# Attention scores of a three-block network: second product over all 128 partitions, index and retention heads issued in pairs

## The chip, the cores and the metric

The kernel runs on one core of a Trainium2 chip. The metric is the device time of one launch in microseconds (us). Before the change three runs took 3308.53, 3309.18 and 3311.11 us; the median is 3309.18.

## What is computed

Three blocks of a network over 512 tokens of 1024 features, batch 1, in float32. The first is a mixer with a linear recurrence, a gated MLP over chunks and a convolutional feed-forward part. The second holds an mLSTM and a differential attention. The third is a gated feed-forward part, a hybrid mixer of three branches (retention, sparse attention, memory attention) and another feed-forward part. The change touches these pieces of the second and third block:

```python
logits = jnp.einsum('bhmqd,bhmkd->bhmqk', qh[:, :, :, q0:end], kh[:, :, :, :end])   # diff_attention, 8 heads x 2 maps, 64 features
p = jax.nn.softmax(logits + bias[None, :, None], axis=-1)
a = p[:, :, 0] - lam * p[:, :, 1]
...
scores = jnp.einsum('bnihd,bnjhd->bnhij', qc, kc) * decay_in[None, None]             # retention, 4 heads, 64 features
...
rel = jax.nn.relu(jnp.einsum('bqhd,bsd->bqhs', qib, ki).astype(jnp.float32))         # index of the sparse attention, 8 heads, 64 features
score = jnp.einsum('bqhs,bqh->bqs', rel, wib.astype(jnp.float32))
_, idx = lax.top_k(score, topk)                                                      # 128 keys per query
logits = jnp.einsum('bqhd,bqkhd->bhqk', qb, k_sel).astype(jnp.float32) * scale       # sparse attention, 8 heads, 64 features
```

## The kernel before

**Parts of a number.** TensorE multiplies float32r numbers, so every float32 operand is split into a high part (ScalarE rounds it) and a low part (VectorE subtracts), and a product is hi·hi + hi·lo + lo·hi, three matmuls into one PSUM tile: `mm3` (L495, L496, L497) for two activations, `dense` (L419, L420, L422) and `dense_n` (L438 to L440) for an activation and a weight. Weights come by DMA 128x1024 at a time and are split on the way: L102 on ScalarE gives `whi`, L107 on VectorE gives `wlo`. Tokens lie along the free dimension, in tiles of [128 features, 512 tokens].

**Heads of 64 features.** A tile of 128 features holds two heads. `stack` prepares them for `product`: on the left ("sl") the head's own 64 partitions hold the high part and the other 64 the low part; on the right ("sr") both halves hold the high part, and the low part is in a tile of its own, "srl" [128, 512], head 0 on partitions 0 to 63 and head 1 on 64 to 127. `product` then needs two matmuls: L532 over 128 partitions gives hi·hi + lo·hi, L533 over the head's 64 partitions adds hi·lo. Two loops use it: `diff_attn` (8 heads, 4 query blocks, 2 maps: 64 products) and `dsa_branch` (4 pairs, 2 halves, 4 query blocks: 32 products). A query block has 128 queries against 256, 256, 384 and 512 keys. After a product VectorE adds the bias and finds the maximum (L1352), ScalarE takes the exponential (L1354), VectorE divides (L1448 to L1450, or L1792 and L1793), TensorE transposes the weights (L1382), ScalarE and VectorE split them (L1390, L1391), and `attn_pv` multiplies them with the values by `mm3`. In `dsa_branch` GpSimd adds the mask to the bias (L1789). `qk_part` makes the stacked q and k of the next head, or of the next pair, from two `dense` products; in `dsa_branch` it is called after half 0 of a pair and stands in the queues beside half 1.

**Index and retention.** `dsa_index` has 8 heads in 4 tiles (m = 0 to 3) and three query blocks for each: 24 times `mm3` over 64 partitions; ScalarE applies the relu (L1722, into "rl") and VectorE sums over the heads (L1725, L536). `ret_branch` has 4 heads and four key blocks for each, 512, 384, 256 and 128 columns wide: 16 times `mm3` over 64 partitions; VectorE multiplies with the decay (L1658) and the result is split into "Ph" and "Pl".

**Order.** Each engine runs its own queue in the order that a scheduler fixed when the program was built; it weighs the dependences, so that `dense` matmuls of later work stand between the steps of an attention head. An instruction waits until the tiles that it reads are written and the buffer that it writes is free. PSUM has 8 banks: 4 buffers "mm" for the dense products and 4 buffers "sd" for scores, transposes, sums over partitions and value products.

Of the kernel before, what the change touches and what calls it, by code (L numbers as in the profile page):

```python
# [9 lines left out]
FT = mybir.dt.float32  # L10
# [6 lines left out]
P = 128  # L17
# [34 lines left out]
class VecLayout:  # L52
    """Columns of the packed [128, n] array of small vectors."""
# [21 lines left out]
class Stream:  # L75
    """Weight tiles in the order in which TensorE takes them, split into two float32r parts."""
# [46 lines left out]
    def prime(self):  # L123
        """Starts the first load."""
# [11 lines left out]
    def get(self, name, k, c0, again=False):  # L136
        """The next tile of the stream, or with again one that is still held."""
# [31 lines left out]
class Act:  # L169
    """An activation in T-layout: hi and lo parts per 128 features, [128, n] each."""  # L170
# [17 lines left out]
class Norm:  # L188
    """Sums over the features of a residual stream that comes tile by tile, then the normalised tiles."""
# [19 lines left out]
    def adder(self, cols):  # L209
        """The engine that adds the tile up: what is close to the end goes to the faster one."""  # L210
# [8 lines left out]
    def warm(self):  # L219
        """Has the table of Sqrt loaded before it is waited for."""  # L220
        self.nc.scalar.activation(self.small(), self.named("q")[:, 0:2], AF.Sqrt)

    def post(self, cols):
        """What may wait until the next products run."""
# [11 lines left out]
    def mod(self, x, k, r, gs, sh, h, cols):  # L236
        """h = x * r * gs + sh, in two parts"""
# [6 lines left out]
    def mod_off(self, x, k, r, gs, sh, h, cols):  # L244
        """mod without VectorE"""
# [9 lines left out]
class NormMod(Norm):  # L255
    """x is kept in DRAM; rms norm, gain, modulation"""
# [53 lines left out]
class NormGain(Norm):  # L310
    """x = rms norm (gain g), kept in DRAM"""
# [20 lines left out]
class NormLayer(Norm):  # L332
    """x = layer norm, kept in DRAM; the mean of tile 0 comes off before the sums are taken"""
# [41 lines left out]
class Kernel:  # L375
# [7 lines left out]
    # ---------------------------------------------------------------- helpers  # L383
# [14 lines left out]
    def xh(self, dt=FT):  # L398
        """One of the [128, 512] slots of the residual stream and its normalised form."""
# [13 lines left out]
    def dense(self, name, c0, K, parts, k0=0, again=False, ks=None):  # L413
        """parts: [(psum, Act)]; psum[m, t] = sum_k w[k, c0 + m] act[k, t]; ks: the part of the k to do now."""
# [9 lines left out]
    def dense_group(self, jobs, a):  # L424
        """jobs: [(psum, name, c0, K)]: the first half of the tokens for all, then the second."""
# [5 lines left out]
    def dense_n(self, name, c0, K, a, pss, ks=None):  # L431
        """pss[b][t, m] = sum_k act[k, 128 b + t] w[k, c0 + m], m < 512."""
# [55 lines left out]
    def last_of(self, engine):  # L488
        """The last instruction so far of an engine."""
# [19 lines left out]
    def stack(self, pool, src, left, bufs=None):  # L509
        """The two heads of src[128, T] (64 features each) for product(): their columns follow each other.  # L510

        left: hi on the head's own partitions, lo on the other half. Otherwise hi on both halves,
        and lo in a tile of its own."""
        nc = self.nc
        a = self.t(pool, [P, 2 * T], "sl" if left else "sr", FR, bufs)
        lo = a if left else self.t(pool, [P, T], "srl", FR, bufs)
        for i in range(2):
# [5 lines left out]
            else:  # L523
                nc.vector.tensor_sub(lo[r, :], src[r, :], a[r, c].bitcast(FT))
                nc.vector.tensor_copy(a[o, c], a[r, c].bitcast(FT))
        return a if left else (a, lo)

    def product(self, ps, l, lc, r, rc, i):
        """ps = l[:, lc]^T r[:, rc] over the features of head i, l and r as stack() makes them."""
        s, mm = slice(64 * i, 64 * i + 64), self.nc.tensor.matmul  # L530
        lc, rl = slice(i * T + lc.start, i * T + lc.stop), slice(i * T + rc.start, i * T + rc.stop)
        mm(ps, l[:, lc], r[0][:, rl], start=True, stop=False)  # L532
        mm(ps, l[s, lc], r[1][s, rc], start=False, stop=True)  # L533
# [4 lines left out]
    def colsum(self, src, cols=FULL):  # L538
        """PSUM [128, n]: the sum over partitions, on every partition."""
# [4 lines left out]
    def rsqrt(self, pool, src, scale, eps, tag="t"):  # L544
        """1 / sqrt(scale * src + eps)"""
# [13 lines left out]
    def log1p_exp_neg_abs(self, pool, y, shape, tag):  # L559
        """log(1 + exp(-|y|)) by 2 atanh(e / (2 + e))."""  # L560
# [17 lines left out]
    # ---------------------------------------------------------------- the residual stream  # L578
# [9 lines left out]
    def keep_x(self, k, cols):  # L588
        """x[k] goes to DRAM, which is where the next residual sum takes it from."""
# [5 lines left out]
    def next_x(self):  # L595
        """x of the last norm becomes the old x."""
# [3 lines left out]
    def residual(self, alloc, scale):  # L600
        """An epilogue: x[m] = psum * scale(m) + old x[m]."""
# [10 lines left out]
    # ---------------------------------------------------------------- whole  # L612
# [1349 lines left out]
```

## Time and profile before

| | |
|---|---|
| three runs | 3308.53, 3309.18, 3311.11 us |
| profiled execution, span from first to last instruction | 3311.8 us |
| TensorE busy | 3227.9 us, 97% |
| VectorE busy | 2038.7 us, 62% |
| ScalarE busy | 1312.3 us, 40% |
| GpSimd busy | 190.9 us, 6% |
| chain that ended last | 82% TensorE, 10% VectorE, 3% DMA, 2% ScalarE |
| mean granted clock of TensorE | 0.987 |

The only time recorded of the profiled execution itself is its span, 2.6 us above the median of the runs. The span of TensorE's work in `diff_attn` is about 1568 to 1792 us, in `dsa_index` 2376 to 2406, in `ret_branch` 2570 to 2639, and in `dsa_branch` 2719 to 2815. A matmul's duration in the trace is that of one passing through the array; matmuls overlap, so what one costs in a stream is the distance from its start to the start of the next.

### The profile page before, as it was taken

How to read it: one execution, taken by the hardware profiler on the slowest of the kernel's cores; microseconds unless marked ns; L12 is line 12 of the kernel's file. 1: busy time of each engine (PE TensorE's matmuls, PEld its weight loads, DVE VectorE, ACT ScalarE, POOL GpSimd, SP SyncE). 2: the span in 40 equal slices, each digit the busy share in tenths (PEclk: the TensorE clock that was granted, in tenths of full speed). 3: DMA queues.
4: the chain of work that ended last, by engine and by line, in shares of the span. 5: the costliest groups of instructions: out<-in, count | busy, mean ns of one | idle time of the engine just before them, and what ended most of it. 6: DMA issues, size and time to landing. Idle time of an engine off the chain costs nothing.

```text
span 3311.8 us, 40039 instructions
## 1 busy us (share of the span) xinstructions
PE 3227.9 (97%) x15534; PEld 2651.9 (80%) x15534; DVE 2038.7 (62%) x3160; ACT 1312.3 (40%) x2010; POOL 190.9 (6%) x264
## 2 busy tenths in 40 slices
PE   8999999999999999999999999999999999989998
PEld 4778788888888888887777888888887777788887
DVE  6996676588738746655777353333796647563334
ACT  4665232344324433433655233222543535342222
POOL 2100000100001000000000010000200002020001
PEclk9999999999999999999999999999999999999999
DMA  5124766433333232232222333333323131333331
GB/s 202 51 64 135 242 219 190 132 98 100 105 111 98 70 102 89 65 101 86 67 86 69 113 115 102 102 109 102 116 81 117 54 109 61 115 103 98 109 109 61
DMA packets 123108, 352.52 MB, mean 106 GB/s; under 512 B 13978, under 2 KB 28668, under 8 KB 122788
## 3 DMA queue, kind: packets, MB, share of 16 engines
q1 hardware_dynamic: 118612, 336.18, 32.2%
q0 software_dynamic: 4304, 13.77, 1.3%
q8 instruction: 122, 2.00, 0.2%
q14 instruction: 70, 0.57, 0.1%
HBM read 337.27 MB, written 16.82 MB: 107 GB/s over the span
## 4 chain that ended last, share of the span: by engine, by line
PE 82%; DVE 10%; DMA 3%; issue 2%; ACT 2%; SPq 0%; POOL 0%; ACTq 0%; DVEq 0%; POOLq 0%
PE mm L420 19%; PE mm L419 19%; PE mm L422 19%; PE sd L422 4%; PE sd L420 4%; PE sd L419 4%; PE mm L439 2%; PE mm L440 2%; PE mm L438 2%; DVE wlo L107 2%; PE sd L495 1%; PE sd L497 1%; PE sd L496 1%; DMA gv<-in_wmod 1%; DVE xh L536 1%
## 5 line engine op out<-in xcount | busy, mean ns | idle before, releaser
L107 DVE TENSOR_TENSOR wlo<-wst,whi 128x1024 fp32r<-128x1024 f32 x496 | 608.9, 1229 | 625.0 <-ACT whi L102 612.0
L102 ACT CAST whi<-wst 128x1024 fp32r<-128x1024 f32 x485 | 509.0, 1051 | 1185.9 <-PE mm L420 739.6
L420 PE MATMUL mm<-xh,whi 128*128 128x512 f32 (+1 forms) x2256 | 861.6, 383 | 15.6 <-DVE xh L536 11.4
L419 PE MATMUL mm<-xh,whi 128*128 128x512 f32 (+1 forms) x2256 | 859.9, 382 | 14.2 <-ACT xh L364 10.6
L422 PE MATMUL mm<-xh,wlo 128*128 128x512 f32 (+1 forms) x2256 | 853.3, 380 | 0.0
L420 PEld LDWEIGHTS mm<-xh,whi 128*128 128x128 f32 x2256 | 431.5, 191 | 96.1 <-DVE xh L536 15.1
L419 PEld LDWEIGHTS mm<-xh,whi 128*128 128x128 f32 x2256 | 430.9, 191 | 95.9 <-ACT xh L364 11.5
L422 PEld LDWEIGHTS mm<-xh,wlo 128*128 128x128 f32 x2256 | 430.0, 191 | 78.1 <-issue 6.2
L419 PE MATMUL sd<-xh,whi 128*128 128x512 f32 (+1 forms) x576 | 215.0, 373 | 0.0
L420 PE MATMUL sd<-xh,whi 128*128 128x512 f32 (+1 forms) x576 | 214.4, 372 | 0.0
L422 PE MATMUL sd<-xh,wlo 128*128 128x512 f32 (+1 forms) x576 | 214.3, 372 | 0.0
L420 PE MATMUL mm<-d,whi 128*128 128x512 f32 (+1 forms) x540 | 187.7, 348 | 0.0
L422 PE MATMUL mm<-d,wlo 128*128 128x512 f32 (+1 forms) x540 | 187.1, 347 | 0.0
L419 PE MATMUL mm<-d,whi 128*128 128x512 f32 (+1 forms) x540 | 187.1, 347 | 0.0
L438 PE MATMUL mm<-whi,xh 128*128 128x512 f32 x336 | 131.8, 394 | 6.1 <-DVE whi L104 3.1
L439 PE MATMUL mm<-wlo,xh 128*128 128x512 f32 x336 | 132.9, 396 | 0.6 <-DVE wlo L107 0.6
L440 PE MATMUL mm<-whi,xh 128*128 128x512 f32 x336 | 131.8, 394 | 0.0
L536 DVE SCALAR_TENSOR_TENSOR t<-t,vec,t 128x441 f32<-128x441 f32 (+2 forms) x176 | 122.6, 701 | 10.0 <-ACT t L1033 5.7
L419 PEld LDWEIGHTS sd<-xh,whi 128*128 128x128 f32 x576 | 109.2, 190 | 18.8
L420 PEld LDWEIGHTS sd<-xh,whi 128*128 128x128 f32 x576 | 108.9, 189 | 18.8
L422 PEld LDWEIGHTS sd<-xh,wlo 128*128 128x128 f32 x576 | 108.8, 189 | 18.7
L1495 DVE TENSOR_TENSOR t<-t,sd 128x512 f32<-128x512 f32 x44 | 30.3, 688 | 143.6 <-PE sd L422 140.0
(487 smaller groups left out, 5224.5 us busy)
## 6 DMA issues: line engine op xcount, KB each, us to landing
wst<-in_w SPq DMA_DIRECT2D x516, 512.0 KB, 3.5
gv<-in_wmod SPq DMA_DIRECT2D x64, 256.0 KB, 3.5
gv<-in_wada SPq DMA_DIRECT2D x48, 256.0 KB, 3.2
t<-xd POOLq DMA_DIRECT2D x40, 256.0 KB, 3.6
xd<-xh SPq DMA_DIRECT2D x72, 128.0 KB, 1.8
wm<-in_wmod SPq DMA_DIRECT2D x32, 256.0 KB, 5.0
tmat<-trow SPq DMA_DIRECT2D x2, 2048.0 KB
tp<-tmat SPq DMA_DIRECT2D x16, 256.0 KB, 2.6
```

The source lines that it names most:

```text
L102: self.after(nc.scalar.copy(hi, st))
L107: self.after(eng.tensor_sub(lo, st, hi.bitcast(FT)))
L419: mm(ps, wh, a.hi[k], start=(k == 0), stop=False)
L420: mm(ps, wh, a.lo[k], start=False, stop=False)
L422: mm(ps, wl, a.hi[k], start=False, stop=(k == K - 1))
L438: mm(ps, a.hi[k][:, s], wh, start=(k == 0), stop=False)
L439: mm(ps, a.hi[k][:, s], wl, start=False, stop=False)
L440: mm(ps, a.lo[k][:, s], wh, start=False, stop=(k == K - 1))
L495: mm(ps, l[0], r[0], start=start, stop=False)
L496: mm(ps, l[0], r[1], start=False, stop=False)
L497: mm(ps, l[1], r[0], start=False, stop=stop)
L536: self.nc.vector.scalar_tensor_tensor(out, in0, s, in1, op0=op0, op1=op1)
```

## The change

Three things.

1. `low_tile` makes one "srl" tile [128, 1024] for each of `diff_attn` and `dsa_branch`; GpSimd zeroes the 64 rows of each half that no head uses (two memsets of 64x512). `stack` writes the low part of the right operand there, head i in columns 512 i to 512 i + 511 on its own 64 partitions. The second matmul of `product` (L539 in the changed file, L533 before) then takes all 128 rows of left and right; the rows of the low part of the left meet zeros. The tile has one buffer and is shared by all heads of the branch, where before there were two buffers.
2. `pair_products` (L546) issues the three matmuls of two heads in turn, head 0 on rows 0 to 63, head 1 on rows 64 to 127, into two "sd" buffers. `dsa_index` uses it for each query block ("rl" has 4 buffers instead of 3), `ret_branch` for each key block: `decayed` makes the scores of both heads ahead of the first head's value product ("Ph" and "Pl" have 2 buffers each instead of 1; cosine and sine lie in the "o" buffers).
3. Comments and descriptions are removed, so that line numbers differ.

In `dsa_branch` the stacked keys of the next pair are written to the shared tile before half 1 of pairs 0 to 2 takes its second product. That product therefore takes the low part of the next pair's keys, and waits for it to be written.

```diff
+    def low_tile(self, pool):
+        z = self.t(pool, [P, 2 * T], "srl", FR)
+        for i in range(2):
+            self.nc.gpsimd.memset(z[64 - 64 * i:128 - 64 * i, i * T:i * T + T].bitcast(FT), 0.0)
+        return z
...
-        lo = a if left else self.t(pool, [P, T], "srl", FR, bufs)
...
-                nc.vector.tensor_sub(lo[r, :], src[r, :], a[r, c].bitcast(FT))
+                nc.vector.tensor_sub(low[r, c], src[r, :], a[r, c].bitcast(FT))
...
     def product(self, ps, l, lc, r, rc, i):
-        s, mm = slice(64 * i, 64 * i + 64), self.nc.tensor.matmul
-        lc, rl = slice(i * T + lc.start, i * T + lc.stop), slice(i * T + rc.start, i * T + rc.stop)
-        mm(ps, l[:, lc], r[0][:, rl], start=True, stop=False)
-        mm(ps, l[s, lc], r[1][s, rc], start=False, stop=True)
+        mm = self.nc.tensor.matmul
+        lc, rc = slice(i * T + lc.start, i * T + lc.stop), slice(i * T + rc.start, i * T + rc.stop)
+        mm(ps, l[:, lc], r[0][:, rc], start=True, stop=False)
+        mm(ps, l[:, lc], r[1][:, rc], start=False, stop=True)
+
+    def pair_products(self, pss, l, lc, r, rc):
+        for a, b in ((0, 0), (0, 1), (1, 0)):
+            for i, ps in enumerate(pss):
+                s = slice(64 * i, 64 * i + 64)
+                self.nc.tensor.matmul(ps, l[a][s, lc], r[b][s, rc], start=(a + b == 0), stop=(a == 1))
...
     def ret_branch(self, h, acc):
-            for hd in range(4):
-                q, k = rot[hd // 2], rot[2 + hd // 2]
...
-                    self.mm3(ps[:, :n], (k[0][r, ks], k[1][r, ks]), (q[0][r, t0:], q[1][r, t0:]), True, True)
...
+            def decayed(pr):
+                pms = [Act(), Act()]
+                for sb in range(4):
...
+                    pss = [self.sd()[:, :n] for _ in range(2)]
+                    self.pair_products(pss, rot[2 + pr], slice(t0, t0 + P), rot[pr], slice(t0, T))
...
     def dsa_index(self, h, pm, mem):
-                for half in range(2):
-                    hd = 2 * m + half
...
-                        self.mm3(ps[:, :n], (q[0][r, qs], q[1][r, qs]), (ki[0][r, :n], ki[1][r, :n]), True, True)
-                        rl = self.t(p2, [P, T], "rl", bufs=3)
+                for blk in range(1, 4):
+                    n = (blk + 1) * P
+                    pss = [self.sd()[:, :n] for _ in range(2)]
+                    self.pair_products(pss, q, slice(blk * P, n), ki, slice(0, n))
+                    for half, ps in enumerate(pss):
+                        hd = 2 * m + half
+                        rl = self.t(p2, [P, T], "rl", bufs=4)
...
     def dsa_branch(self, h, acc, mask):
+            low = self.low_tile(p)
+
             def qk_part(pr):
...
-                    qk.append(self.stack(p, ps, not w, 2))
+                    qk.append(self.stack(p, ps, not w, 2, low))
```

In `diff_attn` the order of every queue stays as it was, but for the names. It changes at three places that the prediction speaks of.

TensorE's queue in `dsa_branch`, start of half 1 of pair 0, before (numbers behind an underscore are those of the buffers; sd_21768 and sd_21778 are the scores of query blocks 0 and 1, mm_21926 is a dense product of later work):

```order
L497 MATMUL sd_21746<-aTh_21599,v_21592 128x256
L532 MATMUL sd_21768<-sr_21447,sl_21411 128x256
L533 MATMUL sd_21768<-srl_21448,sl_21411 128x256
L532 MATMUL sd_21778<-sr_21447,sl_21411 128x256
L533 MATMUL sd_21778<-srl_21448,sl_21411 128x256
L419 MATMUL mm_21926<-xh_17435,whi_21551 128x512
L420 MATMUL mm_21926<-xh_17436,whi_21551 128x512
```

The same place with the change (sd_21764 and sd_21774 are now the scores, srl_21375 is the one low tile of the branch):

```order
L497 MATMUL sd_21742<-aTh_21596,v_21589 128x256
L538 MATMUL sd_21764<-sr_21445,sl_21409 128x256
L538 MATMUL sd_21774<-sr_21445,sl_21409 128x256
L419 MATMUL mm_21922<-xh_17430,whi_21548 128x512
...
L420 MATMUL mm_21922<-xh_17437,whi_21548 128x512
L539 MATMUL sd_21764<-srl_21375,sl_21409 128x256
L539 MATMUL sd_21774<-srl_21375,sl_21409 128x256
L422 MATMUL mm_21922<-xh_17436,wlo_21550 128x512
```

Eleven dense matmuls now stand between the first and the second products, which are behind the write of the next pair's low part. In pair 1 there are 15 matmuls between them; in pair 2 the order is as before, and in pair 3 there is no next pair.

VectorE's queue at that place with the change (mm_21704 are the next pair's keys, L528 to L531 are `stack`, o_21593 is a value product that half 0 leaves, sd_21764 and sd_21774 are read by L1365, which was L1352):

```order
L528 TENSOR_TENSOR sl_21699<-mm_21668,sl_21699 64x512 x2
L107 TENSOR_TENSOR wlo_22181<-wst_22177,whi_22179 128x1024
L530 TENSOR_TENSOR srl_21375<-mm_21704,sr_21735 64x512
L531 CAST sr_21735<-sr_21735 64x512
L501 TENSOR_TENSOR o_21593<-sd_21742,o_21592 64x512
L530 TENSOR_TENSOR srl_21375<-mm_21704,sr_21735 64x512
L531 CAST sr_21735<-sr_21735 64x512
L1365 ISA sm_21767,nm_21768<-sd_21764,tp_21757 128x128
```

TensorE's second products of half 1 now stand behind both writes of srl_21375; before, they read another buffer, written one pair earlier.

TensorE's queue in `ret_branch` with the change, pair 1 (rot_20149 and rot_20150 are the keys' parts, rot_20237 and rot_20238 the queries'):

```order
L546 MATMUL sd_20595<-rot_20149,rot_20237 128x512
L546 MATMUL sd_20596<-rot_20149,rot_20237 128x512
L546 MATMUL sd_20595<-rot_20150,rot_20237 128x512
L546 MATMUL sd_20596<-rot_20150,rot_20237 128x512
L546 MATMUL sd_20595<-rot_20149,rot_20238 128x512
L546 MATMUL sd_20596<-rot_20149,rot_20238 128x512
L546 MATMUL sd_20615<-rot_20149,rot_20237 128x384
L546 MATMUL sd_20615<-rot_20150,rot_20237 128x384
L546 MATMUL sd_20615<-rot_20149,rot_20238 128x384
```

Only the first key block is issued in turn here; behind it the scheduler puts the two heads apart, with 1 to 27 other matmuls between them. In pair 0 the first two key blocks are in turn and the others apart. The 64-row matmuls of retention make 9 runs where there were 6. In `dsa_index` all 12 pairs stand in turn.

## Rows read from the trace of the kernel before

**Rows 1.** Page, busy time of the engines (us, share of the span, instructions).

```profile
PE 3227.9 (97%) x15534; PEld 2651.9 (80%) x15534; DVE 2038.7 (62%) x3160; ACT 1312.3 (40%) x2010; POOL 190.9 (6%) x264
```

**Rows 2.** Page, chain that ended last, by engine.

```profile
PE 82%; DVE 10%; DMA 3%; issue 2%; ACT 2%; SPq 0%; POOL 0%; ACTq 0%; DVEq 0%; POOLq 0%
```

**Rows 3.** Timeline of PE, diff_attn, first head: start us, duration us, instruction.

```profile
1567.93 0.28 PE L532 MATMUL sd<-sr,sl 128*128 128x256 f32 x1
1568.14 0.38 PE L533 MATMUL sd<-srl,sl 64*128 64x256 f32 x1
1568.45 0.38 PE L532 MATMUL sd<-sr,sl 128*128 128x256 f32 x1
...
1570.34 0.50 PE L419 MATMUL mm<-xh,whi 128*128 128x512 f32 x1
1570.68 0.40 PE L420 MATMUL mm<-xh,whi 128*128 128x512 f32 x1
1570.92 0.40 PE L422 MATMUL mm<-xh,wlo 128*128 128x512 f32 x1
```

**Rows 4.** Timeline of PE, diff_attn, second head: a product of 512 columns, then dense.

```profile
1606.91 0.40 PE L532 MATMUL sd<-sr,sl 128*128 128x512 f32 x1
...
1608.00 0.40 PE L420 MATMUL mm<-xh,whi 128*128 128x512 f32 x1
```

**Rows 5.** Timeline of PE, a dense stream of 256 columns over 128 rows.

```profile
2367.75 0.28 PE L420 MATMUL mm<-xh,whi 128*128 128x256 f32 x1
2367.87 0.28 PE L422 MATMUL mm<-xh,wlo 128*128 128x256 f32 x1
```

**Rows 6.** Weight loads of L532: ns min/median/max; who waited for L533: us, times.

```profile
L532 PEld LDWEIGHTS sd<-sr,sl x96: 186/188/248, 1567.7 to 2814.1; 128*128 128x128 f32 x96
  DVE sm L1352: 21.1, 28
```

**Rows 7.** Windows: length, busy PE, PEld, DVE, ACT, POOL, PEclk, DMA, GB/s.

```profile
1567.93:1584.38 16.45, 16.45 (x68) 11.43 (x66) 13.42 (x42) 9.34 (x25) 0.00 (x0) 1.00 0.25 79
1620.65:1640.75 20.10, 20.10 (x83) 14.38 (x82) 17.04 (x43) 12.24 (x28) 0.00 (x0) 1.00 0.13 39
2749.40:2773.20 23.80, 23.23 (x110) 16.87 (x108) 19.53 (x51) 13.50 (x33) 6.81 (x10) 1.00 0.21 67
```

**Rows 8.** Timeline of DVE, diff_attn, third head: in brackets the idle time before.

```profile
1621.90 0.29 DVE L1352 CUSTOM_DVE_ANT_0 sm<-sd,tp 128x128 f32<-128x128 f32 x1 [0.32 <-PE sd L533]
...
1622.76 0.42 DVE L1352 CUSTOM_DVE_ANT_0 sm<-sd,tp 128x256 f32<-128x256 f32 x1 [0.56 <-PE sd L533]
...
1623.62 0.42 DVE L1352 CUSTOM_DVE_ANT_0 sm<-sd,tp 128x256 f32<-128x256 f32 x1 [0.42 <-PE sd L533]
```

**Rows 9.** Timeline of all engines, dsa_branch, half 1 of pair 1.

```profile
2761.21 0.38 PE L533 MATMUL sd<-srl,sl 64*128 64x256 f32 x1
...
2762.15 0.70 DVE L524 TENSOR_TENSOR srl<-mm,sr 64x512 fp32r<-64x512 f32 x1
...
2768.67 1.48 DVE L1793 TENSOR_SCALAR sm<-sm,sums 128x384 f32<-128x384 f32 x1
...
2770.30 0.52 PE L1382 MATMUL sd<-ident,sm 128*128 128x128 f32 x3 [0.54 <-DVE sums L1792]
```

**Rows 10.** Timeline of all engines, dsa_index, m = 0 and 1.

```profile
2378.90 0.38 PE L495 MATMUL sd<-kih,iq 64*128 64x256 f32 x1 [1.43 <-DVE iwT L1712]
...
2386.00 0.33 PE L497 MATMUL sd<-kih,iq 64*128 64x384 f32 x1
2386.01 0.55 PE L495 MATMUL sd<-kih,iq 64*128 64x256 f32 x2
...
2386.44 1.26 ACT L1722 ACTIVATE rl<-sd 128x256 f32<-128x256 f32 x3
```

**Rows 11.** Windows, columns as in rows 7: dsa_index.

```profile
2375.63:2406.00 30.37, 28.94 (x170) 24.59 (x168) 20.41 (x34) 17.22 (x34) 0.00 (x0) 0.94 0.34 104
```

**Rows 12.** Timeline of PE, end of ret_branch: first matmul of its output product.

```profile
2639.18 0.50 PE L419 MATMUL mm<-o,whi 128*128 128x512 f32 x1 [1.59 <-DVE t L536]
```

More of the change, by code (lines that the diff above doesn't have):

```diff
@@ L223, in post @@
     def post(self, cols):
+        pass
     def rsqrt(self, tag, src, scale, eps, cols):
@@ L507, in split_new, with stack @@
         return hi, lo
-    def stack(self, pool, src, left, bufs=None):
+    def low_tile(self, pool):
[3 more added lines that the diff above has]
+        return z
+    def stack(self, pool, src, left, bufs=None, low=None):
         nc = self.nc
         a = self.t(pool, [P, 2 * T], "sl" if left else "sr", FR, bufs)
-        lo = a if left else self.t(pool, [P, T], "srl", FR, bufs)
         for i in range(2):
@@ L523, in stack @@
             else:
-                nc.vector.tensor_sub(lo[r, :], src[r, :], a[r, c].bitcast(FT))
+                nc.vector.tensor_sub(low[r, c], src[r, :], a[r, c].bitcast(FT))
                 nc.vector.tensor_copy(a[o, c], a[r, c].bitcast(FT))
-        return a if left else (a, lo)
+        return a if left else (a, low)
     def product(self, ps, l, lc, r, rc, i):
-        s, mm = slice(64 * i, 64 * i + 64), self.nc.tensor.matmul
-        lc, rl = slice(i * T + lc.start, i * T + lc.stop), slice(i * T + rc.start, i * T + rc.stop)
-        mm(ps, l[:, lc], r[0][:, rl], start=True, stop=False)
-        mm(ps, l[s, lc], r[1][s, rc], start=False, stop=True)
+        mm = self.nc.tensor.matmul
[7 more added lines that the diff above has]
+                self.nc.tensor.matmul(ps, l[a][s, lc], r[b][s, rc], start=(a + b == 0), stop=(a == 1))
     def stt(self, out, in0, s, in1, op0, op1):
@@ L1618, in ret_branch @@
             p = self.pool("ret", es)
-            cosT, sinT = self.t(p, [P, T], "cos"), self.t(p, [P, T], "sin")
+            cosT, sinT = (self.t(p, [P, T], "o", FT, 8) for _ in range(2))
             nc.sync.dma_start(cosT, ai["rope"][0])
@@ L1646, in ret_branch @@
             o = Act()
-            for hd in range(4):
-                q, k = rot[hd // 2], rot[2 + hd // 2]
-                r = slice(64 * (hd % 2), 64 * (hd % 2) + 64)
-                Pm = Act()
+            def decayed(pr):
+                pms = [Act(), Act()]
                 for sb in range(4):
@@ L1653, in ret_branch @@
                     n = T - t0
-                    ps = self.sd()
-                    ks = slice(t0, t0 + P)
-                    self.mm3(ps[:, :n], (k[0][r, ks], k[1][r, ks]), (q[0][r, t0:], q[1][r, t0:]), True, True)
-                    e = tt()
-                    nc.vector.tensor_mul(e[:, :n], ps[:, :n], dec[:, hd, :n])
-                    hi, lo = self.t(p, [P, n], f"Ph{sb}", FR), self.t(p, [P, n], f"Pl{sb}", FR)
-                    self.split(e[:, :n], hi, lo)
-                    Pm.add(hi, lo)
+                    pss = [self.sd()[:, :n] for _ in range(2)]
+                    self.pair_products(pss, rot[2 + pr], slice(t0, t0 + P), rot[pr], slice(t0, T))
+                    for i, ps in enumerate(pss):
+                        e = tt()
+                        nc.vector.tensor_mul(e[:, :n], ps, dec[:, 2 * pr + i, :n])
+                        hi = self.t(p, [P, n], f"Ph{sb}", FR, 2)
+                        lo = self.t(p, [P, n], f"Pl{sb}", FR, 2)
+                        self.split(e[:, :n], hi, lo)
+                        pms[i].add(hi, lo)
+                return pms
+            for hd in range(4):
+                if hd % 2 == 0:
+                    pms = decayed(hd // 2)
+                Pm = pms[hd % 2]
                 po = self.sd()
@@ L1712, in dsa_index @@
                     nc.vector.tensor_copy(iwT, pw[:, :32])
-                for half in range(2):
-                    hd = 2 * m + half
-                    r = slice(64 * half, 64 * half + 64)
-                    for blk in range(1, 4):
-                        n = (blk + 1) * P
-                        qs = slice(blk * P, n)
-                        ps = self.sd()
-                        self.mm3(ps[:, :n], (q[0][r, qs], q[1][r, qs]), (ki[0][r, :n], ki[1][r, :n]), True, True)
-                        rl = self.t(p2, [P, T], "rl", bufs=3)
+                for blk in range(1, 4):
[5 more added lines that the diff above has]
+                        rl = self.t(p2, [P, T], "rl", bufs=4)
                         nc.scalar.activation(rl[:, :n], ps[:, :n], AF.Relu)
@@ L1752, in dsa_branch @@
             self.bufs[id(p), "sm"] = 5
+            low = self.low_tile(p)
             def qk_part(pr):
@@ L1758, in qk_part @@
                     self.dense("w_in_3", 1536 + w * T + pr * P, KD, [(ps, h)])
-                    qk.append(self.stack(p, ps, not w, 2))
+                    qk.append(self.stack(p, ps, not w, 2, low))
                 return qk
```

## The prediction

> **What bounds the kernel now.** I read the page first. TensorE is busy 97% of the span [rows 1] and holds 82% of the chain that ended last [rows 2]; VectorE, at 62%, is the only other engine with a share of that chain worth naming, 10%. So a gain must make TensorE's queue shorter, and it counts only as far as VectorE delivers what TensorE then asks for sooner. Second, TensorE's timeline where the products stand. The reader is to compare distances between starts, not durations. In a stream of 256-column matmuls over 128 rows the next one starts 0.12 us later [rows 5], with 512 columns 0.24 us later (the last two lines of [rows 3]). In the products, where a matmul over 128 rows and one over 64 follow each other, the distance is 0.21 at the first change and 0.31 from then on [rows 3]. Third, windows over single heads, which show how busy VectorE is in the stretch that would shrink [rows 7]. Fourth, the waits at the edges of the stretches [rows 8 to 12].
>
> **The product over all rows (part 1), on TensorE alone.** From the first L532 of a head to the second dense matmul behind its four products pass 2.75 us [rows 3]. Eight matmuls at 0.12 and one at 0.24 would take 1.20. The four products thus pay 1.55 us for changes of rows, 0.39 each. A product of 512 columns and the dense matmul behind it take 1.09 us [rows 4] where three at 0.24 would take 0.72: 0.37. I take 0.39 for all sizes. With the change no instruction of the product uses 64 rows, so TensorE's queue is 64 x 0.39 = 25.0 us shorter in diff_attn and 32 x 0.39 = 12.5 in dsa_branch (the 96 are counted in [rows 6]). The second matmul itself costs the same over 128 rows: it streams the same columns, and the stream of [rows 5] is over 128 rows.
>
> **What VectorE lets through in diff_attn.** A head's eight products lie between its first L532 and the transposes of query block 3; this stretch would be 8 x 0.39 = 3.1 us shorter. In the first head it is 16.45 us long with VectorE busy for 13.42 [rows 7]; 13.3 would be left, so VectorE just follows. I take heads 1, 4 and 5 like it (0 and 4 come after a gap filled by the values' products) and give the four 3.0 each, 12 us. In the third head the stretch is 20.10 us, VectorE busy 17.04 [rows 7]. TensorE would need 17.0. VectorE's waits for L533 there, 0.32 + 0.56 + 0.42 = 1.3 us [rows 8], vanish; what else it idles are handoffs to ScalarE and back inside its chain, which stay. Between the bare 17.04 and 20.10 - 1.3 = 18.8 I take 18.2, nearer the upper end because of them. So TensorE now waits for VectorE some 1.2 us in each of four such heads (2, 3, 6, 7), and 1.9 of the 3.1 is gained: 7.6 us. Sum for diff_attn 20 us; bounds 8 (VectorE holds every head to 1 us of its 3.1) and 25.
>
> **dsa_branch.** A pair takes 23.80 us with VectorE busy for 19.53 [rows 7]. TensorE already waits 0.54 us for VectorE at the transposes of block 2 in half 1, behind a 1.48 us division [rows 9]. Half 0 can use its 4 x 0.39 = 1.56 us; half 1, held by VectorE, little of it. Against this stands the new wait: in half 1 of pairs 0 to 2 the second product needs the next pair's low part. That write starts at 2762.15 and takes 0.70 us, while the product that now needs it ran at 2761.21 [rows 9]: 1.64 us late. The scheduler fills it with 11 dense matmuls in pair 0 (11 x 0.24 = 2.6 us) and with 15 matmuls in pair 1, and not in pair 2. What is queued behind the waiting matmul is TensorE's whole queue; and the softmax of blocks 0 and 1 starts later, so VectorE, solid behind it, ends later by as much. I put half 1 at -0.4 to +0.4 us, that is zero, and half 0 at 1.5 x 4 = 6: with a little for pair 3, which has no such wait, 6.5 us. Bounds: 12.5, and a loss of 5 if each of three waits is 1.64 and nothing is gained.
>
> **Index in pairs.** One instruction moves beside another only if both halves of the array are used at once. The rows show that this happens: the first matmul of head 1 starts at 2386.01, 0.01 us after one of head 0 at 2386.00 [rows 10]. A tile m has 18 matmuls: 6 x 0.12 + 6 x 0.175 + 6 x 0.24 = 3.2 us (0.175, between the two, is an estimate for 384 columns); in pairs 1.6, and 6.4 over four tiles. But each pair takes two of the four "sd" buffers, so the third pair waits for the relus of the first, and these stood at 2386.44, 1.26 us for three [rows 10]; m = 0 waits for the transposed weights anyway, 1.43 us [rows 10], with 1.4 of the stretch's 30.4 us idle on TensorE [rows 11]. I take 0.35 for each tile, about 1.3 us; bounds 0 and 6.4. The Trainium skill, page "TensorE: Matmul & The Clock Gate", section "Packing small matmuls", gives the span of such a group as that of one matmul plus some 4 ns for each further one. The trace agrees as to the start of two, 0.01 us apart; the sum by that page alone would have 6 us here instead of 1.3, as it knows of no buffers.
>
> **Retention in pairs.** In turn run three key blocks: 512 twice and 384 once, which saves 3 x 0.24 x 2 + 3 x 0.175 = 2.0 us. Three more runs of 64 rows among 128-row matmuls cost 3 x 0.39 = 1.2, and the decayed scores of two heads need four evictions by VectorE before an "sd" buffer is free, which I put at 1.5. That is a loss of 0.7. Against it, 14 more dense matmuls stand ahead of the output product at the end of the branch, 14 x 0.24 = 3.4 us, where TensorE now waits 1.59 for VectorE [rows 12] and then a little more. I take a gain of 1.5 us in all, bounds -2 and +4.
>
> **At nothing.** The four memsets stand on GpSimd, 6% busy [rows 1], at the start of a branch; nobody waits unless the first head's low part does, and the dense products of q and k lie before it. The single low tile in diff_attn must be read before the next head's keys overwrite it; there the next k stands some 10 us behind the last product. Should that cover go, VectorE's write would wait for TensorE, a few tenths each head. Comments cost nothing.
>
> **The sum.** 20 + 6.5 + 1.3 + 1.5 = 29.3 us. The durations are from an execution with a span of 3311.8 us, 2.6 above the median of the runs; taken off the median, 3309.2 - 29.3 = 3280 us.
>
> **The rivals.** First, VectorE follows everywhere: it has 38% of the span idle [rows 1], and the waits of [rows 8] are on TensorE. Then 25 + 10 + 2 to 3 and up to 6 from the index are gained, 36 to 46 us: 3263 to 3273. Against it speak the 17.04 of 20.10 and the wait that is there already in dsa_branch. Second, VectorE and the new wait hold more: diff_attn gains 8 to 18, the sparse attention nothing, index and retention 0 to 4: 3287 to 3301. For it speaks that VectorE is busy 82% of the stretch even in the head that I count in full, and 85% in the third [rows 7]. Third, slower: the distance of 0.31 us is not the change of rows but the weight load, 0.188 us [rows 6], which can't hide under the other matmul of the same PSUM tile. Then both products over 128 rows keep the old distance, nothing is gained, and the new waits cost 1.64 to 4 us in three pairs, 5 to 12; with 1 for retention, 3309 + 9 = 3318. It decides where full-row matmuls follow each other in one PSUM tile at more than 0.25 us for 256 columns. Against it: the dense stream runs at 0.12 with loads of that length, into one tile [rows 5]. The same page of the Trainium skill says that a weight load overlaps matmuls in flight only when the row groups differ, under "What overlaps and what doesn't"; that would be this rival, and [rows 5] contradicts it for this kernel. Fourth, the change doesn't do what it says: the distance falls only to 0.25, 96 products gain 12 us on TensorE, half of it held by VectorE, and the new waits take the rest: 3303 to 3316.
>
> **How the numbers follow.** Forecast (3273 to 3287) 0.60, VectorE follows 0.20, VectorE holds more 0.14, nothing 0.03, slower 0.03. About 0.2%, 6.6 us, is what a measurement of this kernel can tell from no change: faster is below 3302.6 and slower above 3315.8. Faster: 0.60 + 0.20 + 0.14 = 0.94; same 0.03; slower 0.03. The range takes the forecast, nearly all of the first rival and the most of the second: 3264 to 3297.
>
> **What would show it.** In the profile after: L538 and L539 at distances of 0.12 us for 256 columns and 0.24 for 512, and no 64-row matmul in a product; TensorE waiting for VectorE about 1.2 us ahead of the transposes of block 3 in heads 2, 3, 6 and 7, and nowhere in heads 0 and 4; a wait for the low part ahead of L539 in half 1 of pairs 0 to 2; pairs of L546 starting 0.01 us apart, with waits for ScalarE before the third pair; and no wait of 1.59 us ahead of retention's output product. The prediction is wrong if those distances stay at 0.31, or if TensorE waits in dsa_branch for longer than half 0 gains.

## The result, and the profile after

The changed kernel takes 3275.94 us (median of four runs, 3275.03 to 3279.36) against 3310.14 for the kernel before in the same comparison: 34.2 us less, a ratio of 0.9898 with a 95% interval of 0.9887 to 0.9910. The profiled execution took 3279.36 us, its span is 3277.6.

The page of the changed kernel, busy time of the engines and the chain that ended last:

```profile
PE 3187.5 (97%) x15534; PEld 2639.8 (81%) x15534; DVE 2035.1 (62%) x3160; ACT 1310.2 (40%) x2010; POOL 193.6 (6%) x268
...
PE 80%; DVE 11%; DMA 3%; issue 3%; ACT 2%; SPq 0%; POOL 0%; ACTq 0%; DVEq 0%; POOLq 0%
```

TensorE has as many matmuls as before [rows 1] and is busy 40 us less; its share of the chain fell by two points [rows 2]. Where the time went is best seen between two matmuls that both kernels have: dense matmuls of the same weight tile, counted from the start of the program. The table gives the differences to the kernel before, worked out from starts in the traces of the profiled executions, one each; the last column names the kernels by what they change, which the next section tells.

| kernel | diff_attn (437.7 us between two dense matmuls) | retention, first score to a later dense matmul (116.28) | an index tile, first to last of 18 matmuls, m = 1 (2.79) | dsa_branch (142.0) |
|---|---|---|---|---|
| the change | -23.0 | -3.55 | 2.53 | -6.7 |
| product alone | -22.9 | +0.02 | 2.79 | -6.7 |
| index in pairs alone | -0.1 | +0.02 | 2.53 | 0.0 |
| retention in pairs alone | -0.1 | -3.58 | 2.70 | -0.1 |
| retention, both heads first, not in turn | 0.0 | -3.56 | 2.78 | -0.1 |
| retention, pair 0 alone | -0.1 | -2.27 | 2.79 | 0.0 |
| retention, pair 1 alone | -0.1 | -3.30 | 2.79 | 0.0 |
| change, own low part | -23.1 | -3.56 | 2.53 | -7.0 |
| change, division on ScalarE | -23.1 | -3.58 | 2.53 | -9.9 |
| change, third index pair in other buffers | -23.2 | -3.54 | 1.46 | -6.7 |
| change, own low part and division on ScalarE | -23.2 | -3.54 | 2.54 | -10.6 |
| before, 64-row products grouped | -9.5 | +0.03 | 2.80 | +0.1 |

So of the 34.2 us diff_attn gave 23.0, the sparse attention 6.7, retention 3.6 and the index three times 0.26, 0.8: 34.1. Outside these stages single profiles differ by up to 5 us from one another with nothing changed there, most of it in the first 1000 us. Around the index too they differ by more than the index gained: m = 0 took 5.28 us in the change against 4.71 before, and 6.28 in the kernel of the product alone, whose index is that of before.

**The distances.** TensorE's timeline of the changed kernel at the place of [rows 3]:

```profile
1568.18 0.28 PE L538 MATMUL sd<-sr,sl 128*128 128x256 f32 x1
1568.30 0.28 PE L539 MATMUL sd<-srl,sl 128*128 128x256 f32 x1
1568.42 0.28 PE L538 MATMUL sd<-sr,sl 128*128 128x256 f32 x1
...
1569.13 0.39 PE L419 MATMUL mm<-xh,whi 128*128 128x512 f32 x1
1569.36 0.40 PE L420 MATMUL mm<-xh,whi 128*128 128x512 f32 x1
```

The distance is 0.12 us, as in the dense stream of [rows 5], and the dense matmul that follows pays nothing either. From the first product to the second dense matmul pass 1.18 us instead of 2.75.

**VectorE in the third head.** Its timeline, at the place of [rows 8], and the window over the same stretch as in [rows 7]; then the window over pair 1 of dsa_branch, from its first product to that of pair 2:

```profile
1616.26 0.43 DVE L1365 CUSTOM_DVE_ANT_0 sm<-sd,tp 128x256 f32<-128x256 f32 x1 [0.36 <-PE sd L539]
...
1623.58 0.69 DVE L501 TENSOR_TENSOR al<-t,ah 128x512 fp32r<-128x512 f32 x1
1624.24 0.29 DVE L1404 TENSOR_TENSOR aTl<-sd,aTh 128x128 fp32r<-128x128 f32 x1
...
1631.03 0.74 DVE L549 SCALAR_TENSOR_TENSOR sm<-sm,sums,sm 128x512 f32<-128x512 f32 x1
```

```profile
1614.93:1632.05 17.12, 17.12 (x84) 14.13 (x82) 16.18 (x43) 12.25 (x28) 0.00 (x0) 1.00 0.11 27
2720.72:2743.53 22.81, 21.79 (x114) 16.94 (x112) 19.29 (x52) 13.38 (x33) 6.78 (x10) 1.00 0.21 70
```

The stretch of the third head shrank from 20.10 to 17.12 us. Behind 1616.26 no row of VectorE has an idle time in brackets any more: its queue is solid, and its last division ends at 1631.77, 0.28 us ahead of the transposes at 1632.05. Before, it idled at three handoffs from ScalarE in the later part of this stretch:

```profile
1630.73 0.69 DVE L501 TENSOR_TENSOR al<-t,ah 128x512 fp32r<-128x512 f32 x1 [0.23 <-ACT ah L500]
...
1633.07 0.42 DVE L1391 TENSOR_TENSOR aTl<-sd,aTh 128x256 fp32r<-128x256 f32 x1 [0.20 <-ACT aTh L1390]
...
1638.93 0.56 DVE L1391 TENSOR_TENSOR aTl<-sd,aTh 128x384 fp32r<-128x384 f32 x1 [0.38 <-ACT aTh L1390]
```

With the change TensorE is busy through the whole stretch: the gain was let through, with little to spare.

**TensorE's waits in dsa_branch.** From the view of waits, TensorE alone, over the seven halves of dsa_branch from the first product to that of the last half: first the kernel before, then the change.

```profile
PE sd L1382 <- DVE sums L1792: 2.1, 4, 0.5
```

```profile
PE sd L1395 <- DVE sums L1813: 2.9, 4, 0.9
PE sd L1395 <- DVE sm L1814: 2.1, 3, 1.0
```

The columns are the waiting instruction, its releaser, us in all, times, the longest. TensorE now waits 5.0 us for VectorE ahead of the transposes, where it waited 2.1. The view of L539's own instructions gives their weight loads (ns min/median/max) and the idle time before them (releaser, us, times); the new wait for the low part is there only once:

```profile
L539 PEld LDWEIGHTS sd<-srl,sl x96: 186/188/192, 1568.2 to 2781.6; 128*128 128x128 f32 x96
  DVE srl L530: 0.5, 1
```

The 0.5 us are the weight load's. The matmul itself came 0.13 us late by it, too little to stand in the view of waits above.

### The profile page after: what moved, and what is told of

It is laid out like the page before. It is cut to its first block, busy times and chain, and to the rows that moved or that the text cites. A ratio compares the mean times of both kernels' runs of the same rounds, so it can differ in the third digit from the quotient of the medians.

```text
span 3277.6 us, 40053 instructions
## 1 busy us (share of the span) xinstructions
PE 3187.5 (97%) x15534; PEld 2639.8 (81%) x15534; DVE 2035.1 (62%) x3160; ACT 1310.2 (40%) x2010; POOL 193.6 (6%) x268
## 4 chain that ended last, share of the span: by engine, by line
PE 80%; DVE 11%; DMA 3%; issue 3%; ACT 2%; SPq 0%; POOL 0%; ACTq 0%; DVEq 0%; POOLq 0%
PE mm L420 19%; PE mm L419 19%; PE mm L422 18%; PE sd L420 4%; PE sd L422 4%; PE sd L419 4%; PE mm L440 2%; PE mm L439 2%; PE mm L438 2%; DVE wlo L107 2%; DMA gv<-in_wmod 2%; DVE xh L549 1%; PE sd L495 1%; PE sd L496 1%; PE sd L497 1%
```

## The experiments

**1. The product alone.** From the change, index and retention as before:

```diff
-                    self.pair_products(pss, q, slice(blk * P, n), ki, slice(0, n))
+                        self.mm3(ps[:, :n], (q[0][r, qs], q[1][r, qs]), (ki[0][r, :n], ki[1][r, :n]), True, True)
...
-                    self.pair_products(pss, rot[2 + pr], slice(t0, t0 + P), rot[pr], slice(t0, T))
+                    self.mm3(ps[:, :n], (k[0][r, ks], k[1][r, ks]), (q[0][r, t0:], q[1][r, t0:]), True, True)
```

> Part 1 of the change alone (zeroed low tile, second product over 128 rows); index and retention as before. Theory: diff_attn keeps its whole gain of 23.2 us and dsa_branch its 6 to 7, since VectorE still follows: 29 to 31 us under the kernel before, about 3280. Rival: the parts are not independent (retention's changed order brought the later stages their gain), then diff_attn gains 23 and the rest less than 3: about 3285.

Measured: 3281.43 us against 3310.44, ratio 0.9911 (0.9897 to 0.9924), 29.0 us less. The stages that it touches show -22.9 and -6.7, as in the change, and retention +0.02. The parts are independent.

**2. Is it the change of rows?** From the kernel before, in diff_attn:

```diff
-                    for mp in range(2):
-                        ps = self.sd()
-                        self.product(ps[:, :N], q, qs, k, slice(0, N), mp)
+                    pss = [self.sd() for _ in range(2)]
+                    self.products(pss, q, qs, k, N)
+                    for mp, ps in enumerate(pss):
                         e.append(self.softmax_rows(p, ps, nk, tp[:, T - nk:T], sums, mp))
```

> The kernel before, with the 128-row matmuls of both maps of a diff_attn block ahead of the two 64-row ones (the scheduler leaves 18 of 32 blocks so, the others as before). Theory: each change of rows costs 0.18 to 0.2 us; 18 blocks have 2 changes less, and the two 64-row matmuls, on different halves, run beside each other: 18 x 0.36 + 2.6 = 9 us on TensorE, so 7 to 9 us faster. Rival: every 64-row matmul costs its 0.2 to 0.4 us however it stands, and the two don't overlap: 0 to 2 us.

Measured: 3298.65 us against 3311.18, ratio 0.9964 (0.9951 to 0.9976). That is 12.5 us less in the medians, but of the 15.1 us between the two profiles 5.3 arise ahead of diff_attn, where nothing was changed. The stage of diff_attn itself shrank by 9.5 us where 9 were worked out. `products` issues L538 for both maps, then L541 on rows 0 to 63 and 64 to 127. TensorE's timeline of the first head:

```profile
1562.66 0.40 PE L538 MATMUL sd<-sr,sl 128*128 128x256 f32 x2
1562.98 0.39 PE L541 MATMUL sd<-srl,sl 64*128 64x256 f32 x2
1563.30 0.50 PE L538 MATMUL sd<-sr,sl 128*128 128x256 f32 x2
1563.73 0.39 PE L541 MATMUL sd<-srl,sl 64*128 64x256 f32 x2
1564.05 0.50 PE L419 MATMUL mm<-xh,whi 128*128 128x512 f32 x1
```

Two 64-row matmuls together take 0.32 us to the next start, as one did in [rows 3]. The two start 0.004 us apart. So the price belongs to the change of rows, not to each 64-row matmul. The four products of the first two blocks take 1.39 us here, 2.41 before and 0.95 with the change.

**3. Index in pairs alone**, with `pair_products` in `dsa_index` and nothing else of the change.

> Index in pairs alone. Theory: the third pair of a tile waits for ScalarE to free an sd buffer, and the first tile for its transposed weights, so the stretch of 30 us shrinks by about 1 us and the time can't be told from that of the kernel before (0 to 2 us faster). Rival: the buffers don't matter and pairs halve the matmuls: 6.4 us faster.

Measured: 3309.93 against 3310.44, ratio 0.9995 (0.9987 to 1.0004): no difference that can be told. A tile shrinks from 2.79 to 2.53 us, as in the change. TensorE and ScalarE in tile m = 1 of the changed kernel:

```profile
2362.09 0.40 PE L546 MATMUL sd<-kih,iq 64*128 64x256 f32 x2
...
2362.91 0.35 PE L546 MATMUL sd<-kih,iq 64*128 64x384 f32 x2
...
2363.34 1.42 ACT L1741 ACTIVATE rl<-sd 128x256 f32<-128x256 f32 x4
...
2363.78 0.77 PE L546 MATMUL sd<-kih,iq 64*128 64x512 f32 x2 [0.53 <-ACT rl L1741]
```

Matmuls counted x2 ran beside each other. Two pairs of blocks are done in 0.99 us; the third starts at 2363.78, when ScalarE has emptied the first buffers.

**4. The third pair in other buffers.** From the change:

```diff
-                    pss = [self.sd()[:, :n] for _ in range(2)]
+                    pss = [(self.mm() if blk == 3 and m else self.sd())[:, :n] for _ in range(2)]
```

> The change, with the third pair of index tiles 1 to 3 in two mm buffers instead of sd. Theory: the wait of the third pair for ScalarE's relu (0.65 to 0.7 us in each of three tiles) is a wait for a buffer and goes; the tiles shrink from 2.53 to about 1.85 us, 2 us in all, unless the dense products then wait for the mm buffers. Rival: TensorE's next instructions wait for ScalarE instead, as the buffers are needed by what follows: no gain within 1 us.

Measured: 3274.74 us, ratio to the kernel before 0.9893 (0.9879 to 0.9908); a comparison of some us with the change is within the scatter of the runs. The trace is clear: tiles 1 to 3 take 1.46, 1.45 and 1.45 us instead of 2.53, 2.53 and 2.49, which is shorter than the 1.85 that were expected, and from the transposed weights to a dense matmul some 100 us later 97.86 us pass instead of 100.12, 2.3 less. The wait was for a buffer. The same tile:

```profile
2362.39 0.39 PE L546 MATMUL sd<-kih,iq 64*128 64x256 f32 x2
...
2363.38 0.39 PE L546 MATMUL mm<-kih,iq 64*128 64x512 f32 x2
2363.61 0.39 PE L546 MATMUL mm<-kil,iq 64*128 64x512 f32 x2
2363.84 0.40 PE L546 MATMUL mm<-kih,iq 64*128 64x512 f32 x2
2364.16 0.50 PE L419 MATMUL mm<-xh,whi 128*128 128x512 f32 x1
```

Here pairs do what a pair can do. The Trainium skill, page "TensorE: Matmul & The Clock Gate", section "Part 3: Packing small matmuls", gives a group's span as that of one matmul and some 4 ns for each other; this tile agrees with it, the one of experiment 3 doesn't, for the sake of the buffers.

**5. The copy of the transposed index weights on ScalarE**, `nc.scalar.copy(iwT, ...)` for `nc.vector.tensor_copy`, in the change.

> The change, with the copy of the transposed index weights on ScalarE. Theory: the first tile's third wait (2.8 us on TensorE) is the place of this copy in VectorE's queue, behind two weight splits of 1.2 us; it goes, 1 to 2.5 us faster than the change. Rival: ScalarE's relus are what frees the buffers, and the wait stays within 0.5 us.

Measured: 3275.13, ratio 0.9891 (0.9878 to 0.9905), that of the change. Tile 0 shrinks from 5.28 to 3.00 us, but tile 1 grows from 2.53 to 3.73, and tile 0 alone lies between 4.71 and 6.37 us in traces of kernels that don't touch it. TensorE's wait in tile 0, in the change, then here; behind it the wait of tile 1 here, and the window behind tile 1:

```profile
2356.11 0.57 PE L546 MATMUL sd<-kih,iq 64*128 64x384 f32 x1 [2.63 <-DVE iwT L1733]
```

```profile
2354.05 0.44 PE L546 MATMUL sd<-kih,iq 64*128 64x384 f32 x1 [1.08 <-ACT iwT L1733]
...
2361.46 0.50 PE L546 MATMUL sd<-kih,iq 64*128 64x512 f32 x1 [0.74 <-ACT rl L1741]
```

```profile
2362.40:2366.00 3.60, 3.60 (x20) 3.38 (x18) 3.50 (x8) 1.17 (x3) 0.00 (x0) 0.57 0.47 149
```

The wait of tile 0 shrank by 1.55 us, and the time did not follow. In tile 1 the heads of the first two blocks start 0.38 and 0.49 us apart instead of 0.003 and 0.02, and the third pair waits 0.74 us for the relu instead of 0.53. Behind tile 1 the granted clock was 0.57 for 3.6 us, where in the change it was low earlier, 0.81 from 2352.70 to 2358.50. Neither the theory's gain came nor the rival's unchanged wait; why the clock fell where it did was not followed.

**6. Retention in pairs alone, and 7. the same with each head's matmuls together.** The second differs from the first in this:

```diff
-                    self.pair_products(pss, rot[2 + pr], slice(t0, t0 + P), rot[pr], slice(t0, T))
+                    for i, ps in enumerate(pss):
+                        r = slice(64 * i, 64 * i + 64)
+                        k, q = rot[2 + pr], rot[pr]
+                        self.mm3(ps, (k[0][r, t0:t0 + P], k[1][r, t0:t0 + P]), (q[0][r, t0:], q[1][r, t0:]), True, True)
```

> Retention in pairs alone. Theory: 4 to 5 us faster, most of it from the end of the branch, where more dense matmuls now stand between the last head's sums and the output product and cover a wait of 1.6 us and one of 0.9 behind it. Rival: the gain came with the shift of the earlier stages, and retention alone gives under 1.5 us.

> Retention with both heads' scores ahead of the first value product, as in the change, but each head's three matmuls together instead of in turn. Theory: the order at the end of the branch gives 2 to 3 us, and the turns 2.0 us on top in the kernel that has them. Rival: all of it comes from the turns: no gain or a loss here.

Measured: 3308.16 and 3307.57 us against 3310.44, both with a ratio of 0.9991 (0.9982 to 1.0000). By the runs alone this is at the edge of what can be told; the traces give 3.58 and 3.56 us for the stage. So issuing the heads in turn brought no gain, the stages differ by 0.02 us, where 2.0 were expected. The reason is in the timeline of kernel 7. TensorE's queue has the three matmuls of head 0, then the three of head 1:

```
L495 MATMUL sd_20386<-rot_20110,rot_20198 128x512
L496 MATMUL sd_20386<-rot_20111,rot_20198 128x512
L497 MATMUL sd_20386<-rot_20110,rot_20199 128x512
L495 MATMUL sd_20387<-rot_20110,rot_20198 128x512
L496 MATMUL sd_20387<-rot_20111,rot_20198 128x512
L497 MATMUL sd_20387<-rot_20110,rot_20199 128x512
```

And this is what ran:

```profile
2565.75 0.51 PE L495 MATMUL sd<-rot,rot 64*128 64x512 f32 x2
2566.09 0.40 PE L496 MATMUL sd<-rot,rot 64*128 64x512 f32 x2
2566.32 0.40 PE L497 MATMUL sd<-rot,rot 64*128 64x512 f32 x2
2566.55 0.34 PE L495 MATMUL sd<-rot,rot 64*128 64x384 f32 x2
...
2567.82 0.38 PE L495 MATMUL sd<-rot,rot 64*128 64x256 f32 x1 [0.57 <-DVE t L1660]
```

Six matmuls of 512 columns were through in 0.80 us: the first of head 1 started 0.01 us after the first of head 0, before the second of head 0, which stands ahead of it in the queue. The two halves ran beside each other without being told to; they only had to stand next to each other in the queue. So both versions have the gain of the pairs, and both wait for VectorE to free a buffer.

**8 and 9. Which pair brings the gain?** The kernel of 7 with both heads' scores first in pair 0 alone, or in pair 1 alone (the diff is that of pair 0; the other has 1 in its place):

```diff
-            def decayed(pr):
+            def decayed(pr, heads=(0, 1)):
...
-                if hd % 2 == 0:
-                    pms = decayed(hd // 2)
+                if hd // 2 != 0:
+                    pms = decayed(hd // 2, (hd % 2,))
+                elif hd % 2 == 0:
+                    pms = decayed(hd // 2)
```

> The kernel before with both heads' scores ahead of the first value product in pair 0 of retention alone (matmuls not in turn). Theory: the gain of retention, 3.65 us in the trace, is the wait at the end of the branch, which pair 1 decides; so the stage stays as in the kernel before, within 0.5 us. Rival: it comes from both pairs in like parts (scores of two heads under one another's evictions): 1.5 to 2 us less.

> The same for pair 1 alone. Theory: nearly all of the 3.65 us of the stage, 3 us or more. Rival: half of it, 1.5 to 2 us.

Measured: 3308.95 and 3308.21 against 3310.06, ratios 0.9998 (0.9987 to 1.0008) and 0.9992 (0.9981 to 1.0002), no difference that runs can tell; the stage is 2.27 and 3.30 us shorter, together more than the 3.55 of both. What was expected of pair 0 fell, its theory (within 0.5 us) and its rival (at most 2 us); what the theory said of pair 1, 3 us or more, came, and yet the reason behind it, that pair 1 decides alone, did not hold. At the end of the branch the kernel before has two waits, that of [rows 12] and this one, 1.13 us from the matmul before it:

```profile
2642.28 0.50 PE L419 MATMUL mm<-o,whi 128*128 128x512 f32 x1 [0.74 <-ACT o L500]
```

Both are gone with either pair first. With pair 1 first one wait of 0.28 us for ScalarE is left; with pair 0 first there is another in their place, and the one for a buffer at the start that kernel 7 has too:

```profile
2628.02 0.40 PE L422 MATMUL mm<-o,wlo 128*128 128x512 f32 x1
2629.38 0.53 PE L419 MATMUL mm<-xh,whi 128*128 128x512 f32 x1 [0.96 <-ACT bt L1543]
```

The starts in the traces take the stage apart. "Waits" is by how much the distances at waits exceed the stream's, "64 rows" the time from the start of each 64-row matmul to the next start:

| kernel | stage | waits | 64 rows | all else |
|---|---|---|---|---|
| before | 116.28 | 2.65 | 8.61 | 105.02 |
| the change | 112.73 | 0.75 | 7.08 | 104.90 |
| 7, both pairs | 112.72 | 0.74 | 7.10 | 104.88 |
| 8, pair 0 | 114.01 | 1.87 | 7.40 | 104.74 |
| 9, pair 1 | 112.98 | 0.44 | 7.81 | 104.73 |

So of the 3.55 us the waits gave 1.90, and the heads beside each other 1.53, net of the three more runs of 64 rows. Kernels 8 and 9 together gain more than kernel 7 as each removes the same two waits.

**10. The low part of half 1 in two buffers.** From the change, with a low tile of 512 columns for each head:

```diff
-            low = self.low_tile(p)
+            low0 = self.low_tile(p, 0)
+            low1 = [self.low_tile(p, 1, 2) for _ in range(2)]
...
-                    qk.append(self.stack(p, ps, not w, 2, low))
+                    qk.append(self.stack(p, ps, not w, 2, (low0, low1[pr % 2])))
```

Half 1 of pairs 0 to 2 then takes the low part of its own keys.

> The change, with the low part of half 1 in two buffers in dsa_branch, so that the next pair's keys don't overwrite it: half 1 has the right low part and the wait ahead of its second products goes. Theory: VectorE holds half 1 (TensorE waits for it ahead of the transposes), so the time is that of the change within 2 us, 34 to 36 us under the kernel before. Rival: the wait is what keeps dsa_branch from its 12.5 us: 3 to 6 us faster than the change, 37 to 40 under before.

Measured: 3275.93 us, ratio 0.9893 (0.9880 to 0.9907): the time of the change. The stage is 0.3 us shorter. The new wait cost next to nothing, and that three of the eight halves of the change take the low part of the wrong keys gains no time.

**11. The division of dsa_branch on ScalarE.** From the change:

```diff
-                        nc.vector.tensor_scalar(e[:, :nk], e[:, :nk], sums, None, op0=OP.mult)
+                        nc.scalar.activation(e[:, :nk], e[:, :nk], AF.Identity, scale=sums)
```

> The change, with the division of the softmax rows of dsa_branch on ScalarE instead of VectorE. Theory: VectorE's queue is what holds dsa_branch; it is relieved of about 3 us a pair, and the 5 us in which TensorE waits ahead of the transposes shrink by half or more: 2 to 5 us faster than the change, 36 to 39 under before. Rival: ScalarE's handoff only takes the place of VectorE's: no gain, or a loss of 1 to 3 us.

Measured: 3272.88 us, ratio 0.9884 (0.9869 to 0.9899), 3 us under the change in the medians and 3.2 in the stage. The intervals of the two ratios overlap, so the stage decides. The view of waits, over the same seven halves, has one line for the transposes left; the last half has two new ones, where the change has none:

```profile
PE sd L1395 <- ACT sm L1814: 0.8, 1, 0.8
```

```profile
PE mm L419 <- ACT o L500: 0.7, 1, 0.7
PE sd L496 <- DVE aTl L1404: 0.5, 1, 0.5
```

VectorE held dsa_branch: with the division gone from it, TensorE's waits went from 5.0 us to 2.0 in all, and these 3.0 are nearly the 3.2 that the stage gained. The scheduler also moved dense matmuls between the halves, so this is not the division alone.

**12. Both of these together.**

> The change, with its own low part for half 1 (right keys in dsa_branch) and the division of the rows of dsa_branch on ScalarE. Theory: the gains of the two add up as far as VectorE still held half 1: 3 to 4 us faster than the change, 37 to 39 under before, ratio 0.9880 to 0.9888. Rival: with VectorE relieved the low part's wait and the division were the same time seen twice: 3 us, ratio 0.9890.

Measured: 3273.16 us, ratio 0.9892 (0.9876 to 0.9909); the stage is 10.6 us shorter than before, 0.6 more than in 11. By the runs it is level with experiment 11 (36.9 us under the kernel before, a ratio nearer the rival's than the theory's), and it uses the right keys. With the buffers of experiment 4 it might take some 2 us less, an estimate from that experiment; the combination was not run.

## Why the prediction was right, and where its steps were not

The prediction was 3280 us; 3275.9 lies in the range, inside the forecast's own 3273 to 3287. Of the gain 29.3 us were worked out and 34.2 came: diff_attn 3.0 more, retention 2.1 more, dsa_branch 0.2 more, the index 0.5 less.

- *The product on TensorE alone*: right. 25.0 us were worked out for diff_attn, and TensorE lost 23.0 there with no wait for VectorE in it, so a product paid 0.36 us instead of 0.39. Experiment 2 shows that the price is that of a change of rows.
- *What VectorE lets through in diff_attn*: this step failed for the third head and its like, by 3 us in all. I took 18.2 us, as the handoffs to ScalarE and back would stay. They went, and with them the 1.2 us of waiting for VectorE that were to show in each of four heads: in the rows above VectorE idles at no handoff, since its queue always had something older to do. The stretch took 17.12, TensorE's own pace. The first rival, VectorE follows everywhere, was right here. The head's windows show 17.04 us busy before and 16.18 after for the same 43 instructions. 0.32 us of this is the window's edge, which cuts the last row (L522, now L528) 0.57 us in before and 0.25 after; the rest is that rows of VectorE overlap when they follow at once (L1404 begins at 1624.24 while the one before it ends at 1624.27). The busy time before was no lower bound.
- *dsa_branch*: 6.7 against 6.5, right in kind, and so close because errors cancel. The kernel of experiment 10 has as many matmuls in each half as the kernel before, so its halves can be compared, from the first product of one to that of the next: half 0 of the four pairs became 0.93, 1.18, 1.18 and 1.23 us shorter, 4.5 where 6 were put, and half 1 of pairs 0 to 2 0.46, 0.42 and 0.40 where nothing was; the last half gave 1.23 where 0.5 were put. So half 0 gained some 0.3 us a product at most, not 0.39. Experiment 11 shows the hold of VectorE that was forecast, experiment 10 that the new wait is not the cause of it. I had put that wait at nothing within 0.4 us a half; the rival's 1.64 us in three pairs did not come, the trace shows 0.5 once, on a weight load.
- *Index*: 0.8 against 1.3, for the reason given; experiment 4 removes that reason and gets 2.3 us more.
- *Retention*: 3.6 against 1.5, within the bounds; right in kind, with sizes off and one reason wrong. The heads beside each other were to give 2.0 us less 1.2 for three more runs, 0.8, and gave 1.5; the wait for an "sd" buffer was put at 1.5 and took 0.75; the end of the branch was to give 2.2 (the 1.5 and the loss of 0.7) and gave 2.65, with the wait of [rows 12] gone. Wrong was that the turns bring the heads beside each other: TensorE does that by itself once they are neighbours in the queue.
- *The slower rival*: dead. The distance of L538 and L539 is 0.12 us with weight loads of 0.19 us, and loads over the same 128 rows did overlap the matmuls.

## What to carry to other kernels

A matmul over 64 rows between matmuls over 128 costs some 0.36 us more than its columns in diff_attn, twice 0.18. Filling it up with zero rows costs TensorE nothing: matmuls of 256 columns start 0.12 us apart over 128 rows here, and 0.11 us apart over 64 rows where two of these follow each other (2385.41 and 2385.53 in the kernel before). Two heads on the two halves of the array need not be issued in turn: in experiment 7 it was enough that they were neighbours in the queue, with PSUM buffers free. Count the buffers first. Before a stretch on TensorE is shortened, look how solid the queue of the engine that follows is, and at its starts rather than its summed busy time.

## What the runs showed of the hardware

- Matmuls on different halves of the rows overtake in the queue: six queued as head 0, 0, 0, 1, 1, 1 ran in three pairs, 0.01 us apart (experiment 7; and in the kernel before at 2386.00 and 2386.01, [rows 10]). The Trainium skill, page "TensorE: Matmul & The Clock Gate", section "What overlaps and what doesn't", has matmuls in strict order; these rows differ from it.
- A change between 128 and 64 rows costs about 0.19 us, the mean of both directions: in experiment 2 the two groups and the dense matmul behind them take 1.73 us (1562.66 to 1564.39) for 0.96 us of stream (six times 0.12, as two 64-row matmuls count once, and 0.24), so 0.77 for four changes. By the starts of [rows 3] most of it comes with the way back: the way into 64 rows takes 0.09 us above the stream's 0.12 (1567.93 to 1568.14), the way out 0.19 above 0.12 (1568.14 to 1568.45), and the distance behind it still 0.10 above 0.24 (1570.34 to 1570.68).
